# One encoder layer on one core: zeros multiplied at the start, and six pieces of work put elsewhere in the order

## The chip, the cores and the metric

The kernel runs on one core of a Trainium2 chip. A core has engines that work side by side, each through its own queue in order: TensorE (PE, matrix products), VectorE (DVE), ScalarE (ACT), GpSimd (POOL) and SyncE (SP), which only issues transfers. DMA transfers move data between device memory and the core's own memory, and products are summed in banks of a third memory, PSUM. The metric is the device time of one execution in microseconds (us), and the value to forecast is the median over several runs.

## The reference

The layer takes two sequences of 512 tokens with 1024 features, all in float32. Cut to what matters:

```
h    = rms_norm(x, ln1);  proj = h @ w_in
q, k, v, u, g_att, g_ssm = split(proj)
q, k = rms_norm(q, q_gain), rms_norm(k, k_gain)       # per head of 64: 16 query heads, 4 key heads
y_att = windowed_attention(q, k, v, sink, bias, mask) # 128-blocks and their neighbours
y_ssm = s5_branch(u, ...)                             # both directions, then y * sigmoid(gelu(y) @ w_glu + b)
x1   = x + (sigmoid(g_att) * y_att + sigmoid(g_ssm) * y_ssm) @ w_out
y    = x1 + relu(rms_norm(x1, ln2) @ w_up)**2 @ w_down   # 4096 hidden features
```

The state-space branch has 64 groups with 64 states and a scan in each direction.

## The kernel before

**How products are made.** A float32 operand is split in a rounded high part (ACT, a cast: c_hi, w_hi, gc_hi) and the rest (DVE, a subtraction: c_lo, w_lo, gc_lo). Each product is three passes, high x high, high x low, low x high, over eight slices of 128 features: 24 matmuls for one PSUM accumulator. A weight block must be fetched by a DMA (c_raw), cast and subtracted before TensorE can use it. Such a block is handled in two halves of four slices.

**The stages**, in the order of TensorE's stream:

1. *Strips* (lines L319 to L350). Eight strips of transposed rows (xr) and of the weights of keys and values (wr), each 128x512, give head products at L343, 12 matmuls a strip. SP issues the transfers (L325), but the first wr goes through ACT's queue (`load_strip(0, S)`).
2. *Columns* (L190, `products`, `column`). 24 blocks of 128 projected features, u and both gates, are pulled as *units* from a generator by `pull(n)`; one matmul of these is two units, one of the key blocks that follow them (L230, `key_products`) one. A `pull` stands wherever TensorE would have nothing else to do. Between pulls lies the state-space branch: tables of coefficients (DVE, ending in the tile bpre, transposed by TensorE at L605), the inputs to the states (L636), the scan, and the outputs (L748).
3. *Keys* (L230). The last four row blocks, 4 to 7, each a product of 24 matmuls of 256 columns with two weight blocks, the first for slices 0 to 3, the second for 4 to 7. Block 4 brings in the splits of the second weight block while it runs.
4. *Attention* (from L1091). The order of PE, DVE and ACT is written out by hand (`manual_schedule`); a scheduler sets that of Pool. Work goes by query tiles: `project` (L914, 24 matmuls in an accumulator), `square`, `power` (Pool: rq is the mean square to the power -1/2, L926 and L927), `norm` (DVE L931: qn from the accumulator and rq), `turn` (transposes, L936); between tiles one block of values (L121 to L123). In the first tile's turn the squares of the keys of the first four blocks are formed (k_sq, L1120), reduced on DVE (k_ms) and taken to the power -1/2 on Pool (L1122 and L1123, k_rs).
5. *Gated unit* (L128, `columns` in L1312). Units u from 2 to 15, column m = u // 2 for sequence u % 2. The dictionary `columns` says in which unit's turn a half of which later weight column is fetched and split. All engines' orders are written out.
6. *Output projection, then the MLP.* The up products have their own ring of banks (`bank()`, L1533); the front stages share a ring of three accumulators (`acc()`). A ring hands out its buffers in turn, and a new use waits for the last read of the old one. Here both rings stand on the same PSUM memory. Before the output stage, `acc` is called until the count of calls leaves 1 by 3, and six calls of `bank()` are made whose results nobody uses.

Of the kernel before, what the change touches and what calls it, by code (L numbers as in the profile page):

```python
# [12 lines left out]
F32 = mybir.dt.float32  # L13
# [6 lines left out]
P = 128  # L20
D = 1024
# [35 lines left out]
ROUND_MAGIC = 12582912.0  # L57
TWO_PI_1 = 6.28125
# [5 lines left out]
def hybrid_layer(ctx, tc, x, x_t, w_kv, rel, onehot, w_qkv, w_ug, vectors, lam, coefs, w_glu, w_out, ln2,  # L64
# [15 lines left out]
    given = itertools.count()  # L80
    banks_used = [0]

    def acc():
        banks_used[0] = next(given) + 1
        return ps_acc.tile([P, 512], F32, tag="acc", name="acc")
# [133 lines left out]
    def key_products():  # L219
        later = None  # L220
        for t in range(NB, NT):
            if t == NB:
                key_tiles.append(evp.tile([P, 4, N_KV, HD], F32, tag="ev", name="keys"))
            kt = key_tiles[-1][:, t % 4]
            ps = acc()[:, 0:CB]
            for n in range(3 * KT):
                k, p = divmod(n, 3)
                hi, lo = loaded[len(columns) + k // 4]
# [5 lines left out]
                if n == 12 and later:  # L234
                    later()
                if n < 3 * KT - 1:
                    yield 1
            psv = ps.rearrange("p (h d) -> p h d", h=N_KV)
# [44 lines left out]
    with tc.tile_pool(name="ssmc", bufs=1) as sc, tc.tile_pool(name="xin", bufs=1, reuse_waits="tile") as xin:  # L283
# [38 lines left out]
        def load_strip(k, eng=SP):  # L322
            strips[k] = [xin.tile([P, HALF], F32, tag=tag, name=tag, bufs=6) for tag in ("xr", "wr")]
            for tile_, src, e in zip(strips[k], (x_t, w_kv), (SP, eng)):
                e.dma_start(tile_, src[k])  # L325
# [26 lines left out]
        load_strip(0, S)  # L352
# [14 lines left out]
        GP.memset(lbt, 0.0)  # L367
        V.memset(pr[:, 0, :], 1.0)
# [140 lines left out]
        ps = ps_o.tile([P, 512], F32, tag="po", name="line")  # L509
# [20 lines left out]
    with tc.tile_pool(name="hst", bufs=1) as hp:  # L530
# [11 lines left out]
        with tc.tile_pool(name="ssmt", bufs=2) as sp:  # L542
# [124 lines left out]
            pull(116)  # L667
# [165 lines left out]
    with tc.tile_pool(name="att", bufs=2, reuse_waits="tile") as ap, tc.tile_pool(name="attc", bufs=1, reuse_waits="tile") as ac:  # L833
# [257 lines left out]
        with tc.manual_schedule(engines={ET.PE, ET.DVE, ET.Activation}):  # L1091
# [14 lines left out]
            for t in range(4):  # L1106
# [11 lines left out]
                if t == 0:  # L1118
                    k_sq = ap.tile([P, NB, N_KV, HD], F32, tag="ya", name="k_sq")
                    S.activation(k_sq, kn[:, 0:4], AF.Square, scale=HD ** -0.5)  # L1120
                    V.reduce_sum(ms, k_sq.rearrange("p t h d -> p (t h) d"), axis=AX.X)
                    GP.tensor_scalar_add(ms, ms, EPS)  # L1122
                    GP.tensor_tensor(rk, ms, neg_half, op=ALU.pow)  # L1123
                if t == 1:
# [182 lines left out]
    with tc.tile_pool(name="glu", bufs=1, reuse_waits="tile") as gpool, \  # L1307
# [4 lines left out]
        columns = {u: (4 + i // 2, i % 2) for i, u in enumerate((3, 4, 7, 8, 9, 10, 11, 12))}  # L1312
# [51 lines left out]
    with tc.tile_pool(name="rn2", bufs=2, reuse_waits="tile") as rn2:  # L1364
# [119 lines left out]
        while banks_used[0] % 3 != 1:  # L1484
            acc()
# [46 lines left out]
    def bank():  # L1532
        return ps_m.tile([P, HALF], F32, tag="bank", name="bank")  # L1533

    for _ in range(6):
        bank()
# [256 lines left out]
```

## Time and profile before

| | us |
|---|---|
| median of 3 runs | 1460.14 (1459.45 to 1464.28) |
| profiled execution | 1461.13 |
| its span, first to last instruction | 1459.3 |
| TensorE busy | 1439.5 |
| VectorE busy | 1098.9 |
| ScalarE busy | 764.3 |
| Pool busy | 236.2 |

A row of the timeline reads: start, duration, engine, line, operation, tile written <- tiles read, shape, count; in brackets, the engine's idle time before it and the instruction that ended it. "PEld" is the load of a weight, which overlaps the products. A row with a count stands for several instructions on end. SPq and ACTq are the queues in which SP and ACT issue transfers. A row of the list of waits tells what waits, for what, the total, the number of times and the longest. A row of the windows gives a stretch, its length, each engine's busy time with the number of its instructions, the granted TensorE clock (1.00 is full), the DMA engines' busy share and GB/s.

### The profile page before, as it was taken

How to read it: one execution, taken by the hardware profiler on the slowest of the kernel's cores; microseconds unless marked ns; L12 is line 12 of the kernel's file. 1: busy time of each engine (PE TensorE's matmuls, PEld its weight loads, DVE VectorE, ACT ScalarE, POOL GpSimd, SP SyncE). 2: the span in 40 equal slices, each digit the busy share in tenths (PEclk: the TensorE clock that was granted, in tenths of full speed). 3: DMA queues.
4: the chain of work that ended last, by engine and by line, in shares of the span. 5: the costliest groups of instructions: out<-in, count | busy, mean ns of one | idle time of the engine just before them, and what ended most of it. 6: DMA issues, size and time to landing. Idle time of an engine off the chain costs nothing.

```text
span 1459.3 us, 22019 instructions
## 1 busy us (share of the span) xinstructions
PE 1439.5 (99%) x7981; PEld 1226.0 (84%) x7981; DVE 1098.9 (75%) x1985; ACT 764.3 (52%) x1361; POOL 236.2 (16%) x386
## 2 busy tenths in 40 slices
PE   8999999999999999999999999999999999999998
PEld 6788888889999999987788878888888888888887
DVE  6999949995457999988975588777776598475654
ACT  7688861234338887884443355545445444333332
POOL 3144452004244432251100000000000000000000
PEclk9999999999999999999999999999999999999999
DMA  7356549428741533345553245444442993554441
GB/s 277 112 166 182 186 132 340 171 108 291 259 165 47 171 102 102 125 139 173 179 184 114 95 144 183 157 151 144 152 143 103 342 325 111 159 187 147 128 130 58
DMA packets 102204, 240.23 MB, mean 165 GB/s; under 512 B 12330, under 2 KB 25130, under 8 KB 102096
## 3 DMA queue, kind: packets, MB, share of 16 engines
q1 hardware_dynamic: 62160, 139.68, 29.4%
q0 software_dynamic: 16320, 48.28, 10.2%
q10 hardware_dynamic: 23616, 50.87, 9.3%
q8 instruction: 63, 1.03, 0.3%
q14 instruction: 45, 0.37, 0.1%
HBM read 169.02 MB, written 81.82 MB: 172 GB/s over the span
## 4 chain that ended last, share of the span: by engine, by line
PE 87%; DVE 6%; ACT 3%; DMA 1%; issue 1%; POOL 1%; DVEq 0%; ACTq 0%; SPq 0%; POOLq 0%
PE acc L190 16%; PE bank L122 14%; PE bank L121 14%; PE bank L123 14%; PE acc L914 5%; PE acc L123 2%; PE acc L121 2%; PE acc L122 2%; PE acc L128 2%; PE sps L748 2%; PE po L997 2%; PE sps L636 2%; PE sps L965 2%; PE tps L981 2%; PE acc L343 1%
## 5 line engine op out<-in xcount | busy, mean ns | idle before, releaser
L190 PE MATMUL acc<-act,c_hi 128*128 128x512 f32 x768 | 244.1, 395 | 0.0
L122 PE MATMUL bank<-b_lo,a_hi 128*128 128x512 f32 (+1 forms) x449 | 174.7, 389 | 0.0
L123 PE MATMUL bank<-b_hi,a_lo 128*128 128x512 f32 (+1 forms) x449 | 174.5, 389 | 0.0
L121 PE MATMUL bank<-b_hi,a_hi 128*128 128x512 f32 (+1 forms) x449 | 174.5, 389 | 0.0
L190 PEld LDWEIGHTS acc<-act,c_hi 128*128 128x128 f32 x768 | 142.4, 188 | 28.1 <-ACT act L316 0.9
L1649 ACT CAST a_hi<-d_a 128x1024 fp32r<-128x1024 f32 x56 | 59.1, 1055 | 177.9 <-PE bank L122 176.2
L190 PE MATMUL acc<-act,c_lo 128*128 128x512 f32 x384 | 151.2, 394 | 0.0
L121 PE MATMUL bank<-act,act 128*128 128x512 f32 x368 | 143.2, 389 | 2.1 <-ACT act L1410 2.1
L122 PE MATMUL bank<-act,act 128*128 128x512 f32 x368 | 143.2, 389 | 0.0
L123 PE MATMUL bank<-act,act 128*128 128x512 f32 x368 | 143.2, 389 | 0.0
L1650 DVE TENSOR_TENSOR a_lo<-d_a,a_hi 128x1024 fp32r<-128x1024 f32 x56 | 68.5, 1223 | 95.7 <-ACT a_hi L1649 95.7
L914 PE MATMUL acc<-w_hi,act 128*128 128x256 f32 x512 | 115.6, 294 | 1.7 <-DVE qn L931 1.7
L122 PEld LDWEIGHTS bank<-b_lo,a_hi 128*128 128x128 f32 x449 | 84.3, 188 | 18.3 <-DVE b_lo L1650 0.6
L121 PEld LDWEIGHTS bank<-b_hi,a_hi 128*128 128x128 f32 x449 | 84.3, 188 | 17.5
L123 PEld LDWEIGHTS bank<-b_hi,a_lo 128*128 128x128 f32 x449 | 84.3, 188 | 17.1
L914 PEld LDWEIGHTS acc<-w_hi,act 128*128 128x128 f32 x512 | 88.2, 192 | 5.7 <-DVE qn L931 1.9
L190 PEld LDWEIGHTS acc<-act,c_lo 128*128 128x128 f32 x384 | 72.2, 188 | 14.0 <-DVE c_lo L181 0.2
L121 PEld LDWEIGHTS bank<-act,act 128*128 128x128 f32 x368 | 69.1, 188 | 16.8 <-ACT act L1410 2.5
L975 ACT ACTIVATE p<-p,nmx 128x257 f32<-128x257 f32 (+1 forms) x128 | 72.1, 564 | 19.8 <-DVE nmx L969 17.6
L128 PE MATMUL acc<-act,gc_hi 128*128 128x512 f32 x256 | 81.2, 395 | 1.0 <-ACT gc_hi L780 1.0
L123 PEld LDWEIGHTS bank<-act,act 128*128 128x128 f32 x368 | 69.1, 188 | 14.5
L122 PEld LDWEIGHTS bank<-act,act 128*128 128x128 f32 x368 | 69.1, 188 | 14.2
(356 smaller groups left out, 3422.7 us busy)
## 6 DMA issues: line engine op xcount, KB each, us to landing
d_a<-a_scr SPq DMA_DIRECT2D x56, 512.0 KB, 3.6
raws<-in_w_up_dram SPq DMA_DIRECT2D x32, 512.0 KB, 4.1
a_scr<-t ACTq DMA_DIRECT2D x64, 256.0 KB, 3.0
k<-in_w_down_dram SPq DMA_DIRECT2D x32, 512.0 KB, 6.0
c_raw<-in_w_ug_dram SPq DMA_DIRECT2D x48, 256.0 KB, 3.6
ct_scr<-ctab POOLq DMA_DIRECT2D x16, 512.0 KB, 4.6
ctab_in<-ct_scr POOLq DMA_DIRECT2D x16, 512.0 KB, 6.3
a_scr<-a ACTq DMA_DIRECT2D x32, 256.0 KB, 2.0
```

The costliest lines, as they stand in the source:

```text
L121: PE.matmul(ps, a[0], b[0], start=first, stop=False)
L122: PE.matmul(ps, a[0], b[1], start=False, stop=False)
L123: PE.matmul(ps, a[1], b[0], start=False, stop=last)
L128: PE.matmul(ps, w[wi][:, k, :], rows[yi], start=k + p == 0, stop=k == KT - 1 and p == 2)
L190: PE.matmul(ps, w[wi][:, k, :], hT[s][hi][:, k, :], start=n == 0, stop=n == 3 * KT - 1)
L636: PE.matmul(ps[:, i * P:(i + 1) * P], bm[:, ri, g, :], u_sb[:, gp * SH + g, :], start=True, stop=True)
L748: PE.matmul(o, ctab[:, g0 % SI + g, ri, 0:T * CH], st[:, ri, g].rearrange("p s k -> p (s k)"), start=False, stop=ri == 1)
L914: PE.matmul(self.ps, hT[sq][act][:, k, col:col + P], w[:, k % 4, :], start=i == 0, stop=i == 3 * KT - 1)
L965: PE.matmul(ps[:, 0:self.nk], qs, kk[:, self.k0 * P:self.k1 * P], start=i == 0, stop=i == 1)
L975: S.activation(p, p, AF.Exp, bias=self.nmx[:, h:h + 1], scale=-1.0, accum_out=self.sums[:, h, self.qb:self.qb + 1])
L1649: S.copy(hi, src)
L1650: V.tensor_sub(lo, src, hi.bitcast(F32))
```

## The change

Seven edits:

- The first wr is issued by SP, directly behind the first xr; ACT issues it no longer.
- VectorE clears a 128x128 tile, and TensorE multiplies it by itself 16 times (WARM) ahead of the first strip. Nobody reads the products.
- 140 units are pulled ahead of the tables instead of 116.
- Key blocks 4 and 5 are both computed with the first weight block before either uses the second; blocks 6 and 7 stay as they were. The hook `later` of the previous block is called at matmul 17 instead of 12.
- In the attention stage Pool's order is written out too. The squares of the keys go to another ring (tag "p" instead of "ya"), and k_rs is taken in the second tile's turn instead of the first's.
- Halves of the gate columns are fetched and split in each of the units 3 to 10, instead of 3, 4, and 7 to 12.
- The calls of `acc` and `bank` whose results nobody uses are gone, and one product of the bias table (`line`) takes its bank from the ring `acc` instead of a pool of its own.

```diff
@@ -55,6 +55,7 @@
 LN2_HI = 0.693359375
 LN2_LO = -2.12194440e-4
 ROUND_MAGIC = 12582912.0
+WARM = 16
 TWO_PI_1 = 6.28125
 TWO_PI_2 = 0.0019350051879882812
 TWO_PI_3 = 3.0199159819567e-07
@@ -77,11 +78,7 @@
     ps_o = front.enter_context(tc.tile_pool(name="ps_o", bufs=1, space=PSUM))
     opers = ExitStack()
 
-    given = itertools.count()
-    banks_used = [0]
-
     def acc():
-        banks_used[0] = next(given) + 1
         return ps_acc.tile([P, 512], F32, tag="acc", name="acc")
 
     def tps():
@@ -217,24 +214,27 @@
         return [products(w, s, finish, i > 0 and s == (i == 1)) for s in range(NSEQ)], store
 
     def key_products():
-        later = None
-        for t in range(NB, NT):
-            if t == NB:
+        later, banks = None, {}
+        for t, half in ((4, 0), (5, 0), (4, 1), (5, 1), (6, 0), (6, 1), (7, 0), (7, 1)):
+            if not key_tiles:
                 key_tiles.append(evp.tile([P, 4, N_KV, HD], F32, tag="ev", name="keys"))
-            kt = key_tiles[-1][:, t % 4]
-            ps = acc()[:, 0:CB]
-            for n in range(3 * KT):
+            if not half:
+                banks[t] = acc()[:, 0:CB]
+            ps, kt = banks[t], key_tiles[-1][:, t % 4]
+            for n in range(half * 12, half * 12 + 12):
                 k, p = divmod(n, 3)
-                hi, lo = loaded[len(columns) + k // 4]
+                hi, lo = loaded[len(columns) + half]
                 act, wt = [(0, hi), (0, lo), (1, hi)][p]
                 PE.matmul(ps, hT[t // 4][act][:, k, (t % 4) * P:(t % 4 + 1) * P], wt[:, k % 4, :],
                           start=n == 0, stop=n == 3 * KT - 1)
                 if t == NB and n in (2, 6):
                     split(n // 6)
-                if n == 12 and later:
+                if n == 17 and later:
                     later()
                 if n < 3 * KT - 1:
                     yield 1
+            if not half:
+                continue
             psv = ps.rearrange("p (h d) -> p h d", h=N_KV)
             S.activation(kt, psv, AF.Square, scale=HD ** -0.5)
             ms = small.tile([P, N_KV], F32, tag="ms", name="ms")
@@ -319,10 +319,10 @@
 
         strips, heads = {}, []
 
-        def load_strip(k, eng=SP):
+        def load_strip(k):
             strips[k] = [xin.tile([P, HALF], F32, tag=tag, name=tag, bufs=6) for tag in ("xr", "wr")]
-            for tile_, src, e in zip(strips[k], (x_t, w_kv), (SP, eng)):
-                e.dma_start(tile_, src[k])
+            for tile_, src in zip(strips[k], (x_t, w_kv)):
+                SP.dma_start(tile_, src[k])
 
         def split_strip(k):
             xr, wr = strips[k]
@@ -349,7 +349,7 @@
                 GP.dma_start(kv_scr[:, t], kv)
 
         S.dma_start(vec, vectors)
-        load_strip(0, S)
+        load_strip(0)
         S.dma_start(lam_sb, lam)
         lr, li, ldt = [lam_sb[:, i] for i in range(3)]
         load_strip(1)
@@ -365,6 +365,11 @@
         GP.dma_start(rel_sb[0:N_BUCKETS, :], rel)
         GP.dma_start(oh_sb, onehot)
         GP.memset(lbt, 0.0)
+        running = xin.tile([P, D], F32, tag="rn_junk", name="running")[:, 0:P]
+        V.memset(running, 0.0)
+        idle = tps()
+        for _ in range(WARM):
+            PE.matmul(idle[:, 0:P], running, running, start=True, stop=True)
         V.memset(pr[:, 0, :], 1.0)
         V.memset(pi[:, 0, :], 0.0)
         sn, sh = c64("sn"), c64("sh")
@@ -506,7 +511,7 @@
         GP.tensor_tensor(dmask, ident[:, 0:CH], ident[:, 32:32 + CH], op=ALU.add)
         for gk in (2, 3):
             GP.tensor_tensor(dmask, dmask, ident[:, gk * 32:gk * 32 + CH], op=ALU.add)
-        ps = ps_o.tile([P, 512], F32, tag="po", name="line")
+        ps = acc()
         PE.matmul(ps[0:N_HEADS, :], rel_sb, oh_sb, start=True, stop=True)
         S.copy(ln_sb, ps[0:N_HEADS, :])
         GP.dma_start(line_one, ln_sb)
@@ -664,7 +669,7 @@
                 pending.insert(0, all_lags)
 
             pending = []
-            pull(116)
+            pull(140)
             for c in range(KT):
                 tables(c)
                 if c == 1:
@@ -1088,7 +1093,7 @@
             return halves
 
 
-        with tc.manual_schedule(engines={ET.PE, ET.DVE, ET.Activation}):
+        with tc.manual_schedule(engines={ET.PE, ET.DVE, ET.Activation, ET.Pool}):
             pull(phase["units"] - 3 * KT)
             SP.dma_start(kn[:, 0:4], kv_scr[:, :, 0])
             w_q = whole_block(w_qkv[Q_BLK], wq, "ya", 2)
@@ -1116,12 +1121,12 @@
                 rows = new
                 rows_block(w_v, NB + t, v_evac)
                 if t == 0:
-                    k_sq = ap.tile([P, NB, N_KV, HD], F32, tag="ya", name="k_sq")
+                    k_sq = ap.tile([P, NB, N_KV, HD], F32, tag="p", name="k_sq", bufs=3)
                     S.activation(k_sq, kn[:, 0:4], AF.Square, scale=HD ** -0.5)
                     V.reduce_sum(ms, k_sq.rearrange("p t h d -> p (t h) d"), axis=AX.X)
+                if t == 1:
                     GP.tensor_scalar_add(ms, ms, EPS)
                     GP.tensor_tensor(rk, ms, neg_half, op=ALU.pow)
-                if t == 1:
                     V.tensor_mul(kn[:, 0:4], kn[:, 0:4],
                                  rk.rearrange("p (t h) -> p t h", t=NB)[:, :, :, None].to_broadcast([P, NB, N_KV, HD]))
                     kd = key_copies(0, 0)
@@ -1309,7 +1314,7 @@
         parts_of(0)
         parts_of(1)
         load_gates(2)
-        columns = {u: (4 + i // 2, i % 2) for i, u in enumerate((3, 4, 7, 8, 9, 10, 11, 12))}
+        columns = {u: (4 + i // 2, i % 2) for i, u in enumerate(range(3, 11))}
         late_raw = []
 
         def small_piece(half, k):
@@ -1481,8 +1486,6 @@
 
         xb, owed = [], None
         order.enter_context(tc.manual_schedule(engines={ET.PE}))
-        while banks_used[0] % 3 != 1:
-            acc()
         x1s = [load_rows_of(sq, 0) for sq in range(NSEQ)]
         SP.dma_start(ln2_bc, ln2.to_broadcast([P, D]))
         for sq in range(NSEQ):
@@ -1531,9 +1534,6 @@
 
     def bank():
         return ps_m.tile([P, HALF], F32, tag="bank", name="bank")
-
-    for _ in range(6):
-        bank()
 
     with tc.tile_pool(name="up", bufs=2, reuse_waits="tile") as fp:
         def product(a, b, w=None):
```

SP's queue at the start of the program (xr rows, wr weights of the strips, xt rows for the norm), before:

```order
L325 DMA xr<-in_x_t_dram 128x512 x2
L325 DMA wr<-in_w_kv_dram 128x512
L325 DMA xr<-in_x_t_dram 128x512
L325 DMA wr<-in_w_kv_dram 128x512
L298 DMA xt<-in_x_dram 128x1024
```

And with the change:

```order
L325 DMA xr<-in_x_t_dram 128x512
L325 DMA wr<-in_w_kv_dram 128x512
L325 DMA xr<-in_x_t_dram 128x512
L325 DMA wr<-in_w_kv_dram 128x512
L325 DMA xr<-in_x_t_dram 128x512
L325 DMA wr<-in_w_kv_dram 128x512
L298 DMA xt<-in_x_dram 128x1024
```

The first wr moved from ACT's queue to the second place of SP's. On TensorE the stream of the changed kernel starts so, at the same place (running is the cleared tile, wh and wl the parts of wr):

```order
L372 MATMUL tps<-running 128x128 x16
L343 MATMUL acc<-wh,act_106 128x512 x3
L343 MATMUL head<-wh,act_106 128x512
L343 MATMUL acc<-wh,act_107 128x512 x3
L343 MATMUL head<-wh,act_107 128x512
```

Only the first row is new. Pool, in the first query tiles of the attention stage (ms and rq belong to a query tile, p to the scores, kd is a copy of keys), before:

```order
L957 COPY p<-vec 128x4
L926 TENSOR_SCALAR ms<-ms 128x4
L927 TENSOR_TENSOR rq<-ms,neg_half 128x4
L1122 TENSOR_SCALAR k_ms<-k_ms 128x16
L1123 TENSOR_TENSOR k_rs<-k_ms,neg_half 128x16
L926 TENSOR_SCALAR ms<-ms 128x4
L927 TENSOR_TENSOR rq<-ms,neg_half 128x4
L883 COPY kd<-kn 128x512
L926 TENSOR_SCALAR ms<-ms 128x4
L927 TENSOR_TENSOR rq<-ms,neg_half 128x4
```

And with the change (five lines further down in the file):

```order
L931 TENSOR_SCALAR ms<-ms 128x4
L932 TENSOR_TENSOR rq<-ms,neg_half 128x4
L962 COPY p<-vec 128x4
L931 TENSOR_SCALAR ms<-ms 128x4
L932 TENSOR_TENSOR rq<-ms,neg_half 128x4
L1128 TENSOR_SCALAR k_ms<-k_ms 128x16
L1129 TENSOR_TENSOR k_rs<-k_ms,neg_half 128x16
L888 COPY kd<-kn 128x512
L931 TENSOR_SCALAR ms<-ms 128x4
L932 TENSOR_TENSOR rq<-ms,neg_half 128x4
```

k_ms and k_rs stood ahead of the second tile's rq and now stand behind it, still ahead of the third's. VectorE in the gated unit, around units 5 and 6 (gc_lo is the low part of half a weight column, ga and gs belong to the gates, yy to the gelu), before:

```order
L781 TENSOR_TENSOR gc_lo<-c_raw,gc_hi 128x512
L825 TENSOR_TENSOR ga<-ga,gs 128x512
L826 TENSOR_TENSOR ga<-ga,at 128x512
L807 TENSOR_TENSOR yy<-act_7366,act_7367 128x8x64
L808 TENSOR_TENSOR gs<-gs,yy 128x512
L831 TENSOR_TENSOR act_8304<-ga,act_8303 128x512
L825 TENSOR_TENSOR ga<-ga,gs 128x512
L826 TENSOR_TENSOR ga<-ga,at 128x512
L807 TENSOR_TENSOR yy<-act_7366,act_7367 128x8x64
L808 TENSOR_TENSOR gs<-gs,yy 128x512
L831 TENSOR_TENSOR act_8302<-ga,act_8301 128x512
L825 TENSOR_TENSOR ga<-ga,gs 128x512
```

And with the change:

```order
L786 TENSOR_TENSOR gc_lo<-c_raw,gc_hi 128x512
L830 TENSOR_TENSOR ga<-ga,gs 128x512
L831 TENSOR_TENSOR ga<-ga,at 128x512
L812 TENSOR_TENSOR yy<-act_7385,act_7386 128x8x64
L813 TENSOR_TENSOR gs<-gs,yy 128x512
L836 TENSOR_TENSOR act_8323<-ga,act_8322 128x512
L786 TENSOR_TENSOR gc_lo<-c_raw,gc_hi 128x512
L830 TENSOR_TENSOR ga<-ga,gs 128x512
L831 TENSOR_TENSOR ga<-ga,at 128x512
L812 TENSOR_TENSOR yy<-act_7385,act_7386 128x8x64
L813 TENSOR_TENSOR gs<-gs,yy 128x512
L836 TENSOR_TENSOR act_8321<-ga,act_8320 128x512
```

The gap of two units without a gc_lo is filled, so that the later ones each stand earlier by two units.

## The prediction

> **What bounds the kernel now.** I read the page's shares first, then the chain of work that ended last, then the list of what TensorE waits for.
>
> ```profile
> PE 1439.5 (99%) x7981; PEld 1226.0 (84%) x7981; DVE 1098.9 (75%) x1985; ACT 764.3 (52%) x1361; POOL 236.2 (16%) x386
> PE 87%; DVE 6%; ACT 3%; DMA 1%; issue 1%; POOL 1%; DVEq 0%; ACTq 0%; SPq 0%; POOLq 0%
> ```
>
> TensorE is busy 99% of a span of 1459.3 us and carries 87% of the chain. It runs its matmuls in order, so time comes only from gaps between matmuls and from stretches at a slower clock. The change removes no product; it can win only what TensorE loses, and this view shows where that is:
>
> ```profile
> PE acc L343 <- ACT act L332: 6.4, 1, 6.4
> PE bank L121 <- ACT act L1410: 2.1, 1, 2.1
> PE acc L914 <- DVE qn L931: 1.7, 1, 1.7
> PE acc L128 <- ACT gc_hi L780: 1.0, 1, 1.0
> ```
>
> Columns are what waits, for what, total us, times, longest. The ends of matmuls are modelled some 0.15 us late, so I count a gap from one start to the next, less the usual spacing. The profiled execution took 1461.13 us, 1.83 more than its span and 0.99 more than the median of 1460.14; the sum below is made against 1459.3, and carried over with +1.83 and -0.99.
>
> **The start.**
>
> ```profile
> 0.73 0.86 SPq L325 DMA_DIRECT2D xr<-in_x_t_dram  x2
> 0.84 0.11 DVE L368 MEMSET pr<- 128x64 f32 x1
> 1.17 0.45 ACTq L325 DMA_DIRECT2D wr<-in_w_kv_dram  x1
> 5.63 0.72 ACT L332 ACTIVATE act<-xr,vec 128x512 fp32r<-128x512 f32 x1 [1.31 <-DMA xr<-in_x_t_dram]
> 5.85 0.43 DVE L333 CAST wh<-wr 128x512 fp32r<-128x512 f32 x1 [4.82 <-DMA wr<-in_w_kv_dram]
> 6.42 1.62 PE L343 MATMUL acc<-wh,act 128*128 128x512 f32 x3 [6.42 <-ACT act L332]
> 11.46 0.86 PE L343 MATMUL acc<-wh,act 128*128 128x512 f32 x3
> 14.26 0.86 PE L343 MATMUL acc<-wh,act 128*128 128x512 f32 x3
> ```
>
> The first weights and the second rows, issued side by side by two engines, land together at about 5.8. Strip 0 then takes 11.46 - 6.42 = 5.04 us for its 12 matmuls, a later strip 14.26 - 11.46 = 2.80: TensorE starts at half rate and comes to full rate about 4.75 us after its first matmul (the spacing changes at 11.17). Behind the first rows in one queue, the weights should land some 1.2 us sooner (between the 3.4 of the first rows, read off the activation that follows them, and 5.6), so strip 0 could start near 4.9.
>
> It won't, because of what is put ahead of it: 16 zero products of 128x128. In float32 each is two passes; this row shows 16 passes, eight such products:
>
> ```profile
> 73.94 1.95 PE L636 MATMUL sps<-u_sb,bm 128*128 128x128 f32 x16
> 75.84 1.38 PE L605 MATMUL tps<-ident,bpre 128*128 128x128 f32 x8
> ```
>
> 1.90 us between the two starts, 0.119 a pass, and 0.238 at half rate. The zeros can begin when VectorE has cleared their tile, about 1.05 (an estimate: its clear of pr runs at 0.84, and the new one stands ahead of it). If full rate comes 4.75 us after the start as before, 20 of the 32 passes are slow and 12 fast: end at 1.05 + 4.75 + 1.43 = 7.23, strip 0 done at 10.03, gain 1.4. If it comes after only 1.5, the end is 1.05 + 1.5 + 26 x 0.119 = 5.6, strip 0 done at 8.4, gain 3.0. If zeros do not wake the clock at all, 32 x 0.238 ends at 8.67 and strip 0, slow, at 13.7: a loss of 2.2. I take **1.8**, nearer the measured delay. So the zeros, and not the weights' transfer, will set the start. The strips and columns behind it can follow 1.8 sooner: VectorE, which feeds them, has 5.3 us free between 30 and 60 (row below).
>
> [...]
>
> **Tables.** At 68, 76 and 85 us eight transposes of bpre wait for VectorE in their middle; later they don't:
>
> ```profile
> 67.68 1.39 PE L605 MATMUL tps<-ident,bpre 128*128 128x128 f32 x8
> 85.29 1.38 PE L605 MATMUL tps<-ident,bpre 128*128 128x128 f32 x8
> 136.04 1.04 PE L605 MATMUL tps<-ident,bpre 128*128 128x128 f32 x8
> 30.00:60.00 30.00, 24.70 (x74) 1.00 0.25 83
> 70.00:160.00 90.00, 89.44 (x174) 1.00 0.57 173
> ```
>
> The last two rows are VectorE's busy time in two stretches: 5.3 us idle from 30 to 60, hardly any from 70 to 160, where it sets the pace. Three times 0.34 is 1.0 us. Pulling 24 more units puts 12 more projection matmuls ahead (at 0.227 each, 2.7 us of TensorE work), and so TensorE arrives later than bpre. It takes these 12 from the fill between later steps, where TensorE has at least 1.4 us in hand by my reading of the later waits. But each column half split earlier costs VectorE 0.7 ahead of bpre, so part may return. I take **0.95**, bounds 0 and 1.0.
>
> **Keys.** The first key block's matmuls meet the second half of its weights before these are split:
>
> ```profile
> 401.26 0.28 PE L230 MATMUL acc<-c_lo,act 128*128 128x256 f32 x1
> 401.38 0.28 PE L230 MATMUL acc<-c_hi,act 128*128 128x256 f32 x1
> 401.92 0.38 PE L230 MATMUL acc<-c_hi,act 128*128 128x256 f32 x1 [0.26 <-ACT c_hi L180]
> 402.64 0.39 PE L230 MATMUL acc<-c_lo,act 128*128 128x256 f32 x1 [0.34 <-DVE c_lo L181]
> ```
>
> The first step is the usual 0.12, the next two are 0.54 and 0.72: 1.02 lost. Now block 4 and 5 both use the first half first, so the second is needed 12 x 0.12 = 1.44 later. Gain **1.0** (0.8 to 1.0). The later steps are unchanged in number; two accumulators are open instead of one, of three.
>
> **Power on the Pool engine.**
>
> ```profile
> 421.68 2.92 POOL L1123 TENSOR_TENSOR k_rs<-k_ms,neg_half 128x16 f32<-128x16 f32 x1
> 424.54 0.28 PE L123 MATMUL acc<-w_hi,act 128*128 128x256 f32 x1
> 425.00 1.04 POOL L927 TENSOR_TENSOR rq<-ms,neg_half 128x4 f32<-128x4 f32 x1
> 426.07 0.42 DVE L931 TENSOR_TENSOR qn<-acc,rq 128x256 f32<-128x256 f32 x1 [3.69 <-POOL rq L927]
> 426.55 0.39 PE L914 MATMUL acc<-w_hi,act 128*128 128x256 f32 x1 [1.74 <-DVE qn L931]
> 427.60:431.00 3.40, 3.40 (x18) 3.39 (x17) 2.40 (x3) 0.00 (x0) 1.47 (x1) 0.50 0.00 0
> 429.00 1.47 POOL L883 COPY kd<-kn 128x512 f32<-128x512 f32 x1 [2.96 <-DVE kn L1125]
> ```
>
> Tile 2's accumulator is Tile 1's, which VectorE frees with qn, after Pool's rq, after Pool's k_rs of 2.92. TensorE loses 426.55 - 424.54 - 0.12 = 1.89. Then its granted clock (third from the end in the window's row, behind each engine's busy time) is 0.50 for 3.40 us: 16 matmuls at 0.21 instead of 0.12, 1.5 more. With k_rs behind Tile 1's rq, that rq ends about 423.75 and qn at 424.25, before 424.66: no wait. What is late next is Tile 2: k_rs ends about 427.2, kn, va and kd follow at 1.22, 1.22 and 1.47, and Tile 2's own rq comes behind kd, its qn at some 431.85, while TensorE wants Tile 3's accumulator at about 431.1. I leave 0.7 there (0 to 1.0). Net 1.89 + 1.5 - 0.7 = **2.7**; bounds 0.9 (the clock drops again) and 3.4.
>
> [...]
>
> **Gate columns.**
>
> ```profile
> 713.07 0.33 SPq L779 DMA_DIRECT2D c_raw<-in_w_glu_dram  x1
> 715.28 0.40 PE L128 MATMUL acc<-act,gc_lo 128*128 128x512 f32 x1
> 716.64 0.73 PE L128 MATMUL acc<-act,gc_hi 128*128 128x512 f32 x2 [0.96 <-ACT gc_hi L780]
> 718.10 0.50 PE L128 MATMUL acc<-act,gc_lo 128*128 128x512 f32 x1 [0.73 <-DVE gc_lo L781]
> ```
>
> 1.36 and 1.46 against 0.23 and 0.46: 2.1 lost to a column half that was fetched only at 713.07. With a half at each of u = 3 to 10, column 5 is split at u = 5 and 6 (done about 710, needed from 712.4). Gain **2.1**, bounds 1.2 (gc_lo late still) and 2.1.
>
> **The PSUM ring.**
>
> ```profile
> 851.38 0.69 DVE L1449 TENSOR_TENSOR f_sum<-acc,f_sum 128x512 f32<-128x512 f32 x1
> 853.57 0.39 PE L123 MATMUL acc<-act,act 128*128 128x512 f32 x1
> 855.28 0.68 DVE L1449 TENSOR_TENSOR f_sum<-acc,f_sum 128x512 f32<-128x512 f32 x1
> 856.11 0.47 PE L121 MATMUL bank<-act,act 128*128 128x512 f32 x1 [2.15 <-ACT act L1410]
> ```
>
> The list blames ACT's cast, but that was issued for later; the bank is freed by the last f_sum add, which ends at 855.97. TensorE loses 856.11 - 853.57 - 0.23 = 2.31. Without the six skipped banks, the first new product gets a bank freed one add earlier (851.38 on), so the wait goes: **2.3**, bounds 0.5 (the next bank waits instead) and 2.3. Behind it TensorE has no gap to the end, so this stays.
>
> **Sum.** 1.8 + 0.95 + 1.0 + 2.7 + 2.1 + 2.3 = 10.85: span 1448.45, profiled 1450.3, median **1449.3**. The low bounds (-2.2, 0, 0.8, 0.9, 1.2, 0.5) give 1.2, the high ones (3.0, 1.0, 1.0, 3.4, 2.1, 2.3) 12.8.
>
> **Rivals.**
> (1) *Zeros don't wake TensorE*, since nothing toggles: the start loses 2.2 instead of gaining 1.8; 1453.3. For it: no row of this profile multiplies only zeros. Against: rate changed here some 4.75 us after work began, with no sign of data playing a part.
> (2) *Waits move.* VectorE is full from 70 to 160, so tables keep their 1.0; Tile 3 waits 1.0 and the clock halves again (gain 0.9); the next bank waits (gain 0.5): 1.8 + 0 + 1.0 + 0.9 + 2.1 + 0.5 = 6.3, 1453.8. For it: each replaced wait has a successor within 1.5 us.
> (3) *The change does not do what it says in the rings*: the count of banks is not what I make it, so up and keys keep their waits: 10.85 - 3.3 = 7.55, 1452.6.
> (4) *Slower.* Gate halves at u = 7 to 10 fill a two-deep ring of weights. ACT, in order, sits at the cast of column 7 until TensorE has read column 5, and gate_out, behind it on ACT, frees the accumulator TensorE needs. If that release came 3.3 us later than I place it, TensorE would stand for a unit of 24 matmuls, 5.5 us, at each of two or three units: 11 to 16.5 lost against 8.75 won elsewhere: 1462 to 1468. From two such units on it decides the sign. Against: I place gate_out about 3.3 us ahead of its need.
>
> **How the numbers follow.** My forecast 0.58, (1) 0.12, (2) 0.16, (3) 0.10, (4) 0.04. A measurement of this kernel tells some 0.3%, 4.4 us, from no change: faster means under 1455.8. The first four cases lie below it save for combinations of (1) with (2): faster 0.87, same 0.10, slower 0.03. The range takes the forecast with its high bounds (1447.3, and a little beyond for small gaps elsewhere) and reaches past (1) to (3): 1446 to 1455.
>
> **What would show it.** Right: strip 0's second strip starts near 9.7; L605 rows of 1.04 at 68 to 86; no 0.5 clock at 427; no wait in L128 and at the first bank product; some 0.7 on qn at Tile 3. Wrong: strip 0 with 0.43 spacing, a new 0.50 stretch, or gaps of L128 at units 9 to 11.

## The result, and the profile after

| | before | changed |
|---|---|---|
| median, us | 1461.25 (4 runs, 1459.45 to 1464.28) | 1451.84 (4 runs, 1450.22 to 1453.75) |
| profiled execution | 1461.13 | 1453.75 |
| its span | 1459.3 | 1451.9 |

The ratio is 0.9934, with a 95% interval of 0.9912 to 0.9956: faster by 0.66%. The forecast was 1449.3, a gain of 10.85, with a range of 1446 to 1455; 9.4 came, and 7.4 in the execution that was profiled, which is the slowest of the four.

The list of TensorE's waits in the changed kernel (what waits, for what, total us, times, longest):

```profile
PE bank L119 <- DVE b_lo L1650: 1.3, 1, 1.3
PE tps L1423 <- DVE rn_xn L1407: 1.1, 1, 1.1
PE tps L372 <- DVE running L369: 1.1, 1, 1.1
PE sps L970 <- DVE nmx L974: 0.9, 2, 0.5
PE po L1002 <- DVE pl L995: 0.7, 2, 0.4
PE sps L753 <- DMA ctab_in<-ct_scr: 0.6, 1, 0.6
PE acc L919 <- DVE qn L936: 0.5, 1, 0.5
...
PE sps L641 <- DMA u_sb<-u_scr: 0.2, 1, 0.2
```

The bank wait on ACT (2.1), the one on gc_hi (1.0), on gc_lo (0.7), on the keys' weights and the long one on qn are gone. Beside the zeros' own wait for their tile (running), four stand there that the list before did not have: b_lo, rn_xn, ctab_in and u_sb. The first strips and the fourth query tile in the timeline of the changed kernel:

```profile
1.08 6.30 PE L372 MATMUL tps<-running 128*128 128x128 f32 x32 [1.08 <-DVE running L369]
4.57 0.43 DVE L333 CAST wh<-wr 128x512 fp32r<-128x512 f32 x1 [3.39 <-DMA wr<-in_w_kv_dram]
7.14 0.94 PE L343 MATMUL acc<-wh,act 128*128 128x512 f32 x3
10.02 0.86 PE L343 MATMUL acc<-wh,act 128*128 128x512 f32 x3
...
429.79 0.39 PE L919 MATMUL acc<-w_hi,act 128*128 128x256 f32 x1 [0.54 <-DVE qn L936]
```

The weights are cast at 4.57 instead of 5.85, and TensorE is busy with zeros till 7.14.

What each stage gave is read by taking the same matmul of TensorE's stream in two profiles: its start in the kernel before, less its start in the other. Nothing but TensorE's own losses stands between two such places. The 12 matmuls that the 140 units bring forward are back at the keys, and no column lies between the tables and the keys, so each compares like with like. How far chance moves a place is seen in line_alone, whose one edit bears on the banks alone: it is 0.54 ahead at strip 1 and 1.05 at the queries.

| kernel | strip 1 (11.46 before) | first transposed queries (421.3) | after the second query tiles (450.0) | before the late gate columns (712.4) | behind them (725.9) | second norm of x1 (775.8) | up products (1090) | last matmul |
|---|---|---|---|---|---|---|---|---|
| changed | 1.45 | 2.20 | 4.86 | 4.80 | 7.48 | 6.12 | 8.88 | 7.37 |
| no_zeros | 1.28 | 2.31 | 4.96 | 4.70 | 7.38 | 6.64 | 8.56 | 9.04 |
| zeros_only | 2.28 | 3.47 | 6.19 | 6.18 | 8.87 | 7.72 | 10.48 | 10.96 |
| nine_zeros | 3.41 | 5.05 | 7.72 | 7.71 | 10.40 | 9.03 | 11.82 | 12.30 |
| pull_116 | 1.39 | 2.85 | 5.52 | 5.44 | 8.13 | 6.16 | 8.91 | 9.19 |
| old_columns | 1.92 | 3.29 | 5.95 | 5.91 | 7.43 | 7.43 | 10.22 | 9.11 |
| power_first | 1.12 | -0.11 | 1.39 | 1.39 | 4.07 | 2.03 | 4.80 | 5.03 |
| six_banks | 1.64 | 2.95 | 5.61 | 5.61 | 8.30 | 7.65 | 10.43 | 10.21 |
| together | 3.54 | 1.74 | 3.54 | 3.59 | 6.28 | 5.24 | 8.01 | 8.49 |
| line_alone | 0.54 | 1.05 | 2.58 | 2.51 | 2.50 | 2.46 | 4.15 | 2.75 |
| pull_alone | 1.11 | 0.74 | 0.77 | 0.73 | 1.24 | 1.24 | 3.45 | 3.26 |
| nine_116 | 2.85 | 4.29 | 6.94 | 6.90 | 9.59 | 7.85 | 10.62 | 11.11 |
| pool_low | 3.15 | 4.75 | 7.41 | 7.41 | 10.10 | 9.39 | 12.17 | 12.65 |

Row 1 in steps: start 1.45; tables, state space and keys together 0.75; Pool's power 2.66; late gate columns 2.68; then 1.36 back at the first norm of x1; 2.76 up to the up products, 2.31 of it at the first bank product; and 1.5 back in the down products. The last loss is at b_lo near 1163 us. Set against the kernel before with the lead of 8.88, the first transfers of that stretch were issued at the same moments to within 0.04, and one of them (d_a, issued at 1128.80 and landed at 1135.56) took 6.76 instead of 5.31; those behind it in the queue came 1 to 2 later. In the table eight of the other twelve end this stretch further ahead than they enter it, while line_alone loses 1.4 and old_columns 1.1. I take it for chance of the transfers, which no experiment here settles.

### The profile page after: what moved, and what is told of

The parts are those of the page before. It is cut to its first block, busy times and chain, and to the rows that moved or that the text cites. A ratio compares the mean times of both kernels' runs of the same rounds, so it can differ in the third digit from the quotient of the medians.

```text
span 1451.9 us, 22089 instructions
## 1 busy us (share of the span) xinstructions
PE 1440.1 (99%) x8013; PEld 1229.0 (85%) x8013; DVE 1099.8 (76%) x1986; ACT 763.2 (53%) x1360; POOL 234.2 (16%) x386
## 5 line engine op out<-in xcount | busy, mean ns | idle before, releaser
L125 PE MATMUL acc<-act,gc_hi 128*128 128x512 f32 x256 | 80.9, 394 | 0.0
```

The costliest lines, as they stand in the source:

```text
L125: PE.matmul(ps, w[wi][:, k, :], rows[yi], start=k + p == 0, stop=k == KT - 1 and p == 2)
```

## The experiments

line_alone and pull_alone are the kernel before with one edit; each of the others is the changed kernel with one edit or a few. Unless an interval is given, the verdict rests on the places in the profile, not on the total, which moves by up to 3.5 us from run to run.

**The start: no_zeros, zeros_only, nine_zeros.**

```diff
-WARM = 16
+WARM = 0
```

> The changed kernel without its 16 zero products; the first weights stay in SP's queue. Theory (full rate comes some 5 us after TensorE's first work, whatever the work): the strips' data are ready at about 5.1, strip 0 runs at half rate until about 10, and strip 1 starts at about 10.2, against 10.02 with the zeros and 11.46 before. So the transfer alone is worth about 1.3, and the zeros next to nothing on top of it. Rival (the zeros carry the gain of the start): strip 1 starts at 11.2 or later.

```diff
-        load_strip(0)
+        load_strip(0, S)      # the first weights on ACT's queue again
```

> The changed kernel with the first weights back on ACT's queue; 16 zero products stay. Theory (the zeros set when strip 0 starts): strip 0 starts at 7.1 and strip 1 at 10.0, as in the changed kernel, since the weights are ready at about 6.4 before the zeros end at 7.14. Rival (the weights' transfer counts): strip 1 starts 1 us later than in the changed kernel, at about 11.

```diff
-WARM = 16
+WARM = 9
```

> The changed kernel with 9 zero products instead of 16. Theory (the zeros need only fill TensorE until the strip's data are there): 18 passes at 0.213 end at 5.0, strip 0 starts at about 5.1, runs at half rate until about 6.3, and strip 1 starts at 8.4 to 8.6, 1.4 to 1.6 sooner than with 16. Rival (fewer zeros put off the release of full rate): strip 1 starts at 10 or later. If the strips behind can follow, the lead of 1.5 is still there at TensorE's first column product.

TensorE's rows at the start of no_zeros (first fence), zeros_only and nine_zeros:

```profile
5.12 1.62 PE L343 MATMUL acc<-wh,act 128*128 128x512 f32 x3 [5.12 <-DVE wh L333]
10.18 0.86 PE L343 MATMUL acc<-wh,act 128*128 128x512 f32 x3
```

```profile
1.07 5.45 PE L372 MATMUL tps<-running 128*128 128x128 f32 x32 [1.07 <-DVE running L369]
6.28 0.95 PE L343 MATMUL acc<-wh,act 128*128 128x512 f32 x3
9.19 0.86 PE L343 MATMUL acc<-wh,act 128*128 128x512 f32 x3
```

```profile
1.08 3.94 PE L372 MATMUL tps<-running 128*128 128x128 f32 x18 [1.08 <-DVE running L369]
5.13 0.94 PE L343 MATMUL acc<-wh,act 128*128 128x512 f32 x3
8.05 0.96 PE L343 MATMUL acc<-wh,act 128*128 128x512 f32 x3
```

Without zeros, strip 1 starts at 10.18, with sixteen at 10.02: once the weights come early, sixteen zeros are worth 0.17 by these two profiles. With the weights late again and sixteen zeros it starts at 9.19, even sooner, since there the zeros ended at 6.28. So the weights' transfer is worth nothing on top of sixteen zeros, and the rival that it counts falls. Both edits fill the same wait. Nine zeros end as the strip's data come, and strip 1 starts at 8.05, 2.0 sooner than with sixteen; the lead stays (3.41 at strip 1, 5.05 at the queries). In time: 1449.0 (1448.8 to 1451.35), ratio 0.9927 (0.9912 to 0.9941), and without zeros 1452.46, ratio 0.9947 (0.9932 to 0.9962). These intervals overlap that of the changed kernel, so the totals alone don't part the three.

From TensorE's first matmul until the granted clock is full it took 5.20 us in the changed kernel (at 6.28 the zeros' passes go from 0.213 us to 0.111), 4.82 in no_zeros, 3.42 in zeros_only, 3.53 in nine_zeros and 4.76 before; over all fourteen profiles 3.27 (together) to 5.87 (power_first). That spread moves the start by itself: with sixteen zeros strip 1 starts at 9.2 after the shortest delay and at 10.3 after the longest. So profiles with about the same delay must be set side by side. With delays of 4.7 to 4.9 strip 1 starts at 8.31 with nine zeros (pool_low), 9.82 with sixteen (six_banks), 10.18 without zeros, and 10.92 and 11.46 with neither edit (line_alone, before). Pairs at 3.4 to 3.5 and at 5.3 to 5.4 give nine zeros 1.1 and 1.5 over sixteen. So of the 2.0 about 1.1 to 1.5 is the edit's, and sixteen zeros are worth 0.4 by such a pair rather than 0.17. The kernel before varies as much: strip 1 starts at 10.35, 10.92 and 11.46 in the three profiles that leave its start as it was (pull_alone, line_alone, before).

**Tables: pull_116, pull_alone.**

```diff
-            pull(140)
+            pull(116)
```

> The changed kernel with 116 units pulled ahead of the tables, as before. Theory (the 12 matmuls were taken from fill that a later stage needed): the waits of about 0.35 in the products of bpre at 67, 75 and 84 us return (1.0 to 1.2 lost), and the waits of the changed kernel in the state-space outputs (0.3 at 331, 0.6 to 0.8 on ctab_in at 385, and 0.28 on u_sb at 134) go, so that TensorE stands within 0.5 of the changed kernel at the keys. Rival (these later waits are chance of the transfers): they stay in about the same size, and TensorE is 1.0 to 1.2 later at the keys.

pull_alone makes the opposite edit in the kernel before (116 to 140).

> The kernel before with one edit: 140 units ahead of the tables instead of 116. Theory (the gain at the tables is given back where the 12 matmuls are missing, and by u_sb, which SP issues later because transfers of weight halves that wait for a buffer stand ahead of it): the three gaps of 0.3 in the products of bpre are gone (1.0 to 1.3 won), a wait of 0.3 to 1 on u_sb appears between 100 and 136 us, and one of 0.3 to 2 on ctab_in near 381; at the keys TensorE is level with the kernel before, within 0.7. Beside it the last accumulator lies in bank 1, so the gap of 2.3 at the first bank product goes. Rival (u_sb and ctab_in were late by the other edits): neither wait, and TensorE 1.0 to 1.3 ahead at the keys.

u_sb, the input of a state-space product, in pull_alone, then what SP issued in the same stretch of the kernel before (second fence), of pull_alone (third) and of the changed kernel (fourth), and ctab_in late in the changed kernel (fifth):

```profile
136.02 0.35 PE L636 MATMUL sps<-u_sb,bm 128*128 128x128 f32 x1 [1.24 <-DMA u_sb<-u_scr]
```

```profile
127.40 0.73 SPq L628 DMA_DIRECT2D u_sb<-u_scr  x1
133.93 1.60 SPq L170 DMA_DIRECT2D c_raw<-in_w_ug_dram  x2
```

```profile
127.69 0.33 SPq L170 DMA_DIRECT2D c_raw<-in_w_ug_dram  x1
128.12 1.12 SPq L628 DMA_DIRECT2D u_sb<-u_scr  x1
129.33 0.86 SPq L170 DMA_DIRECT2D c_raw<-in_w_ug_dram  x1
```

```profile
124.96 0.33 SPq L562 DMA_DIRECT2D bcx<-in_coefs_dram  x1
127.24 0.33 SPq L167 DMA_DIRECT2D c_raw<-in_w_ug_dram  x1
127.67 1.07 SPq L633 DMA_DIRECT2D u_sb<-u_scr  x1
```

```profile
385.55 0.46 PE L753 MATMUL sps<-st,ctab_in 128*128 128x128 f32 x2 [0.57 <-DMA ctab_in<-ct_scr]
```

With 116 units, the changed kernel has gaps of 0.34, 0.13 and 0.29 in bpre's products and no wait on u_sb or ctab_in. From strip 1 to the queries, less 1.02 for the keys where they are changed, the kernels with 116 units gain 0.44 (pull_116), 0.42 (nine_116), 0.58 (pool_low) and 0.51 (line_alone, keys unchanged). Those with 140 gain -0.27 (changed), 0.01 (no_zeros), 0.17 (zeros_only), 0.62 (nine_zeros), 0.35 (old_columns), -2.25 (power_first), 0.29 (six_banks) and -0.37 (pull_alone). The means are 0.49 and -0.18, the second 0.11 without power_first, where ctab_in alone cost 2.0 and 0.5; and the kernel before, with 116, is 0 by definition. So the edit takes its 0.8 to 1.0 at the tables and on the mean loses as much or more behind them, though not each time: nine_zeros gained the most of all.

Firmer than the means is where the waits stand: the products that read u_sb are late by 0.2 to 2.7 in all nine kernels with more than 116 units, and in none of the five with 116. pull_alone shows it with no other edit, late by 1.31, so the rival falls; ctab_in was not late there, against what I expected, but was in five of the seven changed kernels with 140 units (0.3 to 2.0), and why is open.

The reason that the expectation gives for u_sb is not the one that the rows show. SP issues it hardly later: at 128.12 in pull_alone, 6.6 us ahead of its product's place, at 127.40 in the kernel before, 6.8 ahead. But it takes 7.76 us to land instead of 4.83. With 140 units a pair of weight halves stands one u_sb earlier in SP's queue, and so is under way at the same time, where before it was issued only after u_sb had landed; from 127 to 132 the DMA engines move 346 GB/s in pull_alone and 262 in the kernel before, and are busy 99% and 95%. In the changed kernel u_sb takes 6.72. That the company of these transfers is what slows it is read from this overlap; no run tests it by itself. Only in together, below, does SP issue it late as well. In total pull_116 measured 1452.0, ratio 0.9945 (0.9929 to 0.9962), which tells nothing against 1451.84.

**Gate columns: old_columns.**

```diff
-... enumerate(range(3, 11))}
+... enumerate((3, 4, 7, 8, 9, 10, 11, 12))}
```

> The changed kernel with the halves of the gate columns at units 3, 4 and 7 to 12, as before. Theory (in the gated unit VectorE is nearly full, and TensorE's earlier arrival is partly given back at the first norm behind it): the gaps of 0.3, 1.1 and 0.9 at three products of the gated unit return (2.3 to 2.7 lost there), and the wait of 1.1 to 1.3 on rn_xn at about 762 goes, so the loss at the first rn_xn transposes is only 1.0 to 1.6. Rival (the wait on rn_xn is chance of the transfers, or comes from elsewhere in the change): it stays at 0.6 to 1.3, and the loss behind it is 2.3 to 2.7.

The gated unit of old_columns, and then the first norm of x1 in the changed kernel:

```profile
710.66 0.50 PE L125 MATMUL acc<-act,gc_lo 128*128 128x512 f32 x1 [0.70 <-DVE gc_lo L786]
```

```profile
757.43 1.31 DVE L1392 TENSOR_TENSOR f_lo<-f_raw,f_hi 128x512 fp32r<-128x512 f32 x2 [3.24 <-ACT f_hi L1391]
758.66 0.68 DVE L1381 TENSOR_TENSOR x<-acc,x 128x512 f32<-128x512 f32 x1
761.91 1.28 DVE L1407 SCALAR_TENSOR_TENSOR rn_xn<-x,rs,ln_bc 128x1024 f32<-128x1024 f32 x1 [2.58 <-POOL rs L1401]
763.25 0.55 PE L1423 MATMUL tps<-ident,rn_xn 128*128 128x128 f32 x3 [1.12 <-DVE rn_xn L1407]
```

With the old columns one gap of 0.87 came back, not 2.3, and the unit still gained 1.52 over the kernel before; behind it no wait on rn_xn at all (7.43 and 7.43). The changed kernel gains 2.68 and gives 1.36 back. Net 1.32 against 1.52, and 0.6 to 2.0 in the ten profiles with the new columns: these as such were worth nothing that shows. VectorE, which takes its work in order, now waits for gc_hi itself (0.90 and 0.32 at 708 and 719 us in the changed kernel). As expected, the wait on rn_xn belongs to TensorE's early arrival: it is there, with 0.6 to 2.0, in all profiles with the new columns and in none with the old.

That the unit with old columns lost only 1.16 (2.68 - 1.52) of the 2.68 that the kernel before lost there I had not expected. In the kernel before, the 1.13 gap followed a column half that landed late; line_alone and pull_alone lost 1.31 and 1.09 at that place. It is not the transfers' luck: the half takes 2.9 to 3.1 us to land in all three and in old_columns. SP issues it when VectorE has ended the low part of the half before, 2.4 to 2.5 us ahead of the product's place in the three, and 3.6 ahead in old_columns. VectorE is later in the three because it waited once, some 23 us earlier, for the store of the last ya of the attention stage. The same row in the kernel before and in old_columns:

```profile
690.03 1.14 DVE L807 TENSOR_TENSOR yy<-act,act 128x512 f32<-128x512 f32 x1 [1.35 <-DMA mix_scr<-ya]
```

```profile
682.68 1.15 DVE L812 TENSOR_TENSOR yy<-act,act 128x512 f32<-128x512 f32 x1
```

This wait (1.25 to 1.43) stands in these three and in none of the eleven kernels that have k_sq in the other ring. The addresses in the built programs fit: with k_sq gone from the ring "ya", which has two buffers, the last ya lies in the other one, and yy, which takes over the memory of the first, no longer meets it. So more than half of what the gated unit gained most likely belongs to an edit that was listed under Pool. No run makes that edit alone.

**Pool: power_first.** k_rs again in the first tile's turn, Pool's order still written out:

```diff
-                if t == 1:
                     GP.tensor_scalar_add(ms, ms, EPS)
                     GP.tensor_tensor(rk, ms, neg_half, op=ALU.pow)
+                if t == 1:
```

> The changed kernel with k_rs again taken in the first tile's turn, ahead of the second tile's rq on Pool. Theory: TensorE waits 1.9 on qn at the third tile as before, and the wait of 0.74 at the fourth tile goes or stays below 0.3. [...] Rival (Pool's written order in itself, and not the place of k_rs, gave the gain): no wait at the third tile.

The third query tile of power_first, and its window of 3.4 us behind that (stretch, length, busy time by engine, granted clock, DMA share, GB/s):

```profile
426.67 0.39 PE L919 MATMUL acc<-w_hi,act 128*128 128x256 f32 x1 [1.75 <-DVE qn L936]
427.60:431.00 3.40, 3.40 (x31) 3.40 (x30) 2.93 (x4) 1.07 (x2) 1.70 (x2) 1.00 0.02 5
```

The gap is back (1.90 beyond the usual spacing), and the fourth tile has none; the place of k_rs is the cause. But the clock stays at 1.00, with the same gap that ended in 0.50 before. line_alone, which has the gap of 1.90 too, kept the full clock as well (2.58 - 1.05 = 1.53 won there without any edit), while pull_alone lost it. So of the 2.66 about 1.1 (1.89 less the new 0.78) belongs to the edit each time, and 1.5 only where the clock drops. What decides that is open: the list of waits has 1.7 us on qn in all four. The drop is not rare, though: the mean granted clock is 0.998 or less in 14 of the 25 executions of the kernel before that were timed beside the experiments, which takes at least 4.4 us at half rate (an estimate: 0.0015 of 1460, twice), more than the 0.90 and 1.83 at half rate that the profiles of the kernel before and of the changed one have after their last matmul. These 14 took 1461.6 on the mean, the other eleven 1460.0. In the 33 executions of kernels that moved k_rs it is 0.999 or 1.000.

**The banks: six_banks, line_alone.**

```diff
+    for _ in range(6):
+        bank()
```

> The changed kernel with the six unused calls of bank put back; the padding of the accumulators stays out. Theory (the first up product's bank is freed by the last f_sum add): the gap of 2.3 before the first bank product at about 848 returns, no other. Rival (the accumulators' count, and not the six banks, decides): no gap there, or one below 0.5.

```diff
-        ps = ps_o.tile([P, 512], F32, tag="po", name="line")
+        ps = acc()
```

> The kernel before with one edit: the product of the bias table takes its bank from the ring of accumulators. The six unused banks and the padding stay. Theory, formed after six_banks (the first bank product always gets PSUM bank 0, and waits for the last f_sum add only where the last accumulator lies in bank 0; in the kernel before it does, here it lies in bank 2): the gap of 2.3 before the first bank product at about 856 is gone or below 0.5, all else is as before. Rival (the padding's removal is needed too, or the gap has another cause): it stays above 1.5.

The first bank product and the last f_sum add, in six_banks and in line_alone:

```profile
845.53 0.39 PE L120 MATMUL acc<-act,act 128*128 128x512 f32 x1
845.75 0.39 PE L118 MATMUL bank<-act,act 128*128 128x512 f32 x1
...
847.24 0.68 DVE L1454 TENSOR_TENSOR f_sum<-acc,f_sum 128x512 f32<-128x512 f32 x1
```

```profile
851.28 0.39 PE L123 MATMUL acc<-act,act 128*128 128x512 f32 x1
851.50 0.39 PE L121 MATMUL bank<-act,act 128*128 128x512 f32 x1
...
852.99 0.68 DVE L1449 TENSOR_TENSOR f_sum<-acc,f_sum 128x512 f32<-128x512 f32 x1
```

In both TensorE goes on with no gap, a microsecond and a half before the last add begins. The six banks do nothing. The addresses in the built programs say why: the first bank is PSUM bank 0 whether six calls go before it or not. The last accumulator lies in bank 0 in the kernel before, in bank 1 in the changed one, in bank 2 in line_alone, and in bank 1 in pull_alone, whose gap went too. Each edit tried that moved the last accumulator out of bank 0 took this gap away. In line_alone and pull_alone the second bank had 0.44 to wait; no_zeros, where the last accumulator lies as in the changed kernel, showed 0.44 too, the changed kernel nothing.

**All that seemed better: together, nine_116, pool_low.** together has 9 zeros, 128 units, kd and the split of the first values one tile later, and the first up blocks after the first norm:

```diff
+                if t == 2:
                     kd = key_copies(0, 0)
...
-                if t == 2:
+                if t == 3:
                     key_turn(0, 0, kd)
...
+            if t == 0:
+                ws = [up_parts(0, i, ...) for i in range(2)]
```

> The changed kernel with 9 zeros, 128 units ahead of the tables, the copy kd and the split of the first values moved one tile later, and the first two up blocks fetched and split after the first rows' norm instead of ahead of it. Theory: strip 1 starts at 8.0 to 8.6 (1.4 to 2.0 sooner than with 16 zeros); TensorE's waits at tables and state-space outputs come to 0.3 or less more than nothing, against 1.2 to 2; no wait of 0.74 at the fourth query tile; no wait of 1.1 to 1.3 on rn_xn at about 760, since VectorE adds the second half of x1 ahead of f_lo. In all 3 to 5 under the changed kernel: median 1446.5 to 1449. Rival (these gains are given back at the next join, as with the columns): 1449 to 1451.

It gave 1451.5, ratio 0.9931 (0.9917 to 0.9944), above both what the theory and what the rival had. The lead of 3.54 at strip 1 was gone by the queries. u_sb came 2.65 late at 117 us: SP issued it only 4.1 us ahead of its product's place (6.1 in the kernel before), and it took 6.6 to land. The fourth tile's 0.78 went, but the later turn of the keys cost 0.93 and 0.67 at the first scores (kh and kl late, 437 us). And moving the up blocks down in the program changed nothing on VectorE, where the scheduler left f_lo ahead of x; 0.97 was lost on rn_xn.

nine_116 is 9 zeros and 116 units. pool_low is that, with the up blocks' low parts made by Pool:

```diff
-            V.tensor_sub(lo, raw, hi.bitcast(F32))
+            GP.tensor_tensor(lo, raw, hi.bitcast(F32), op=ALU.subtract)
             return hi, lo
```

> The changed kernel with 9 zeros and 116 units ahead of the tables. Theory: strip 1 starts at 8.0 to 8.6; two or three gaps of 0.3 at the tables; no wait on u_sb or ctab_in; the wait on rn_xn near 760 stays at 1 to 2. TensorE 1.5 to 2.5 ahead of the changed kernel: median 1449 to 1450.3. Rival (the 140 units were worth their 1.2 on the whole): 1450.5 or more, slower than with 9 zeros and 140 (1449.0).

> As nine_116, with the low parts of the first two up blocks made by Pool instead of VectorE. Theory (the wait on rn_xn comes from VectorE's order: f_lo, whose data land late, stands ahead of the second half of x1, which TensorE finished 1.4 us before): the wait on rn_xn near 760 falls from 1 to 2 to below 0.3, and TensorE stays that much ahead; median 1448 to 1449. Rival (the norm's own chain over ACT and Pool is the limit): the wait stays above 0.8, and the time is that of nine_116.

nine_116: 1449.51, ratio 0.9924 (0.9910 to 0.9937), with 1.67 lost on rn_xn. It is as the theory had it, and level with nine_zeros and its 140 units (0.9927). pool_low: 1448.56 (1447.38 to 1449.12), ratio 0.9915 (0.9901 to 0.9929), with 0.63 lost there. Pool in pool_low:

```profile
755.08 2.54 POOL L1392 TENSOR_TENSOR f_lo<-f_raw,f_hi 128x512 fp32r<-128x512 f32 x2 [30.18 <-ACT f_hi L1391]
...
757.72 0.23 POOL L1400 TENSOR_SCALAR ss<-ss 128x1 f32<-128x1 f32 x1
...
759.99 1.09 PE L1423 MATMUL tps<-ident,rn_xn 128*128 128x128 f32 x8 [0.47 <-DVE rn_xn L1407]
```

Between these two kernels the move of f_lo took 1.0 off the wait, and all four runs of pool_low were faster than all five of nine_116 beside it. The size rests on one pair of profiles: with f_lo on VectorE the loss there runs from 0.6 to 2.0, and six_banks has 0.65. What is left is Pool, where f_lo holds up ss until 757.62, as it held up x on VectorE. The result lies between the two expectations. pool_low is the fastest kernel of the study, 0.19% under the changed one by the two ratios (0.9915 and 0.9934), though their intervals overlap.

## Why the prediction was right, and where it was not

- *What bounds it* held: every gain came as a gap between matmuls closed, or a slow stretch gone.
- *The start*: 1.8 forecast, 1.45 measured, 1.1 to 2.3 in the kernels with sixteen zeros. The zeros took 6.06 us from first start to strip 0; the working with the delay of before had 6.18. Its first sum, by that delay alone, gave 1.4; the step up to 1.8 for a shorter delay did not come true, the delay was 5.20; no run shows the 1.5 us that the second sum supposed, and the shortest delay was 3.27 (together). Right also that the zeros and not the transfer set the start. The agreement is in part luck: the start of the kernel before moves by 1.1 from profile to profile, and this one was the latest of three. Not drawn from it: fewer zeros are better. Rival (1), that zeros don't wake TensorE, fell: in the changed kernel the passes go from 0.213 to 0.111 us in the midst of them.
- *Tables*: the failed step. "It takes these 12 from the fill between later steps, where TensorE has at least 1.4 us in hand" was read for VectorE and not for the transfers. The weight halves that move with the 12 matmuls are under way together with u_sb, which landed late; ctab_in came late too, and 0.95 became -0.27 from strip 1 to the queries. Rival (2) named this term, for another reason.
- *Keys*: 1.0 forecast; no gap is left in L228, so the 1.02 are won.
- *Pool's power*: 2.7 forecast, 2.66 measured; the wait left at the fourth tile was put at 0.7 and is 0.78. That the price of the slow clock was counted as sure was wrong: 1.5 of it came in two of the four profiles that have the gap.
- *Gate columns*: 2.1 forecast, 2.68 measured, of which 1.36 is given back 37 us later. The number is near by luck: with the old columns 1.52 came as well, and there the late half was cured by the move of k_sq, which the prediction gave no price. That TensorE arrives earlier at what follows went without the question of who is late next. VectorE is, as its busy time in the gated unit of the changed kernel shows (third pair of numbers behind the length), and the same f_lo stands in its order ahead of x whenever TensorE arrives.

```profile
700.00:748.00 48.00, 48.00 (x214) 39.73 (x213) 44.58 (x64) 25.60 (x45) 3.16 (x6) 1.00 0.52 174
```

- *The PSUM ring*: 2.3 forecast, 2.31 measured at the first bank product. Right that the last f_sum add held the bank; wrong that the six skipped calls chose it. The size came from a row, the cause from an assumption on how a ring counts, so that the gap went at all is luck: other parts of the change shifted the accumulators. Rival (3) had the doubt right, and its price not.
- *Not forecast*: 1.5 at b_lo, which I take for chance, and 0.45 won between the second norm and the up products outside the banks.

With the forecast's terms, 1.45 - 0.27 + 1.02 + 2.66 + 1.32 + 2.76 = 8.94 before the loss at b_lo, against 10.85 (2.76 is the 2.31 at the bank and the 0.45). Rival (4), a slower kernel by late gate halves, showed nothing: L125 has no gap in the profile after.

## What to carry to other kernels

Where one engine bounds a kernel, a wait removed is worth what is left of it at the next join (the late gate columns gained 2.68 us here, and 1.36 of it went back at the first norm of x1): look there for the instruction that stands in order ahead of the one that was waited for. Work moved to another stage takes its transfers along, and one that was in time there may then land late: u_sb took 4.83 us to land in the kernel before and 7.76 in pull_alone. An edit that moves one tile to another ring moves all later tiles of the old one, so look which wait has come or gone far behind it (here VectorE's wait of 1.25 to 1.43 us for the store of the last ya). Two edits that fill the same wait should be tried apart: here nine zeros beat sixteen, and the earlier weights gained nothing beside sixteen.

## What was not expected of the hardware

The same gap of 1.9 us of TensorE was followed by 3.4 us at a granted clock of 0.50 in the kernel before and in pull_alone, and by a full clock in power_first and line_alone. The time from the first matmul to the full clock ranged from 3.27 to 5.87 us in fourteen executions. And zeros brought the full clock as other products did: in the changed kernel 5.20 us after the first of them, their passes going from 0.213 to 0.111 us in the midst of the row, against 4.76 us in the kernel before and 4.82 in no_zeros, whose first products are the strips'.
